# The start of a two-layer decoder trunk: products of zeros first, weights by k-tile, small parameters later, a fixed order in the first unit

## The chip, the cores and the metric

The kernel runs on one core of a Trainium2 chip. The metric is the device time of one execution in microseconds (us); the median over several runs is compared. Times inside an execution are counted from the start of the profiled span. Engines are named as in the profile: PE (matrix products; PEld is its weight load), DVE (vector), ACT (activation), POOL, SP (here it only issues transfers).

## The reference, cut to what matters

x is 256 tokens by 1024 features in float32. Two layers follow each other, each of the form below; the mixer is differential attention in layer 0 and a Mamba-2 SSD mixer in layer 1.

```python
h = h + 0.5 * swiglu(rmsnorm(h, ffn1_norm[i]), ffn1_w_gate[i], ffn1_w_up[i], ffn1_w_down[i])
...
h = h + diff_attention(...)      # layer 0; ssd_mixer(...) in layer 1
h = h + memory_cross_attention(rmsnorm(h, xa_norm[i]), mem, ...)
h = h + 0.5 * swiglu(rmsnorm(h, ffn2_norm[i]), ffn2_w_gate[i], ffn2_w_up[i], ffn2_w_down[i])
...
return rmsnorm(h, final_norm)
```

`swiglu(h, g, u, d)` is `(silu(h @ g) * (h @ u)) @ d` with a hidden width of 2816. All that the change touches lies in the first feed-forward block of layer 0 and in what is loaded for later stages.

## The kernel before, in words

Every large product is worked in units. A unit multiplies the activations, 256 tokens held as two halves of 128, by 512 (or 256) columns of weights, over the 1024 features in eight k-tiles of 128. To keep float32 accuracy, both sides are split in a high and a low part, and each product is three matmuls: high by high (L209), high by low weights (L210), low activations by high weights (L211). One unit of 512 columns has 8 k-tiles x 2 halves x 3 = 48 matmuls of 128x512.

Weights arrive through SP in tiles `w` of four k-tiles, 1 MB each (class `W`, L142 to L159), into four buffers. A granule (`Gran`, L161 to L182) covers two k-tiles of them: `split` has ACT copy the high part (`whi`, L180), and DVE subtract it to get the low part (`wlo`, L181; in some later units POOL). High and low parts have four buffers each, and `use` splits two granules ahead of the one that PE works on (`AHEAD = 2`).

The activations are turned by `Norm.turn` (L321): PE transposes 128x128 pieces of `h` (L327) into PSUM tiles `xt`, two k-tiles to a tile, then ACT writes the high part `xh` scaled by the norm's gain (L282), and DVE the low part `xl` (L283). ACT and DVE read one `xt` tile in turn, not at the same time. `square` (L311) sums the squares on ACT for the root mean square, which is first used when the first gate product is evacuated (L521).

The written order is that of a small planner, `Pipe`: each granule moves its clock on by an estimate of PE's time, and `pipe.after(us, f)` writes the instructions of `f` once the clock is there. After that, the compiler's scheduler orders each engine's instructions anew by its own estimates. Engines then work strictly in that order, so that an instruction that waits holds up all that stands behind it on its engine.

At the outset (`begin`, L364): ACT's queue loads the identity and the first gains (L88, L90). SP loads the left half of x (`load_x(0)`: two transfers of 256 KB), 512 KB of the first gate weights (k-tiles 0 and 1), the right half of x, then the other gate weights in pieces of 512 KB, then the up weights. POOL's queue loads five small parameter arrays (L99, L384 to L392): `cst` (masks and rope frequencies), `pos` (positions), `rows` (gains of all later norms), `vec` (SSD parameters) and `lqk` (the lambda vectors of the attention). What needs them is written much later (`rope_tables`, L463; `lam_col`, L451; `nega`, L889), but the scheduler sets some of it very early.

Of the kernel before, what the change touches and what calls it, by code (L numbers as in the profile page):

```python
# [15 lines left out]
P = 128  # L16
# [42 lines left out]
def trunk(ctx, tc, a, out):  # L59
# [34 lines left out]
    def load_x(c):  # L94
        for t in range(2):
            nc.sync.dma_start(h[t][c], a["x"][0, t * P:(t + 1) * P, c * 512:(c + 1) * 512])
    load_x(0)
    cst = const.tile([P, C_W - P], F32, name="cst")
    nc.gpsimd.dma_start(cst, a["cst"][:, P:])  # L99
    triu = cst[:, C_TRIU - P:C_TRIU]  # L100
# [134 lines left out]

    def wide(parts, norm, name, fin, eng=None):
# [15 lines left out]
        units.append(([Gran(k, 2, *((w[k // 4], 0, n) for w, (_, _, n) in zip(ws, parts)),  # L252
                            eng=eng if k == 6 else None) for k in range(0, KT, 2)], run))

# [46 lines left out]
    class Norm:  # L301
# [9 lines left out]
        def square(self, c):  # L311
# [4 lines left out]
            if self.n == 2:  # L316
                s = sm.tile([P, 16], F32, name="nsum", tag="nsum")
                nc.vector.tensor_tensor(s[:, 0:2], self.ss[:, 0:2], self.ss[:, 2:4], op=ALU.add)
                self.col = rpow(s[:, 0:2], 1.0 / D, 2, "rcol")

        def turn(self, c):  # L321
            for i in range(2):
                ps = v2(small_ps("xt"))
                for j in range(2):
                    f = (2 * i + j) * P
                    for t in range(2):
                        nc.tensor.transpose(ps[:, j, t * P:(t + 1) * P], h[t][c][:, f:f + P], ident)  # L327
                for j in range(2):
                    k = 4 * c + 2 * i + j
                    xh = xp.tile([P, S], F32R, name="xh", tag="xh")  # L330
                    xl = xp.tile([P, S], F32R, name="xl", tag="xl")
                    split_act(xh, xl, ps[:, j, :], self.g[:, k:k + 1])
                    self.x.append((xh, xl))

# [28 lines left out]

    def begin(norm):  # L364
        ps0 = small_ps("pcol0")
        nc.tensor.transpose(ps0[:, :KT + 1], rows0, ident[:KT + 1, :KT + 1])
        nc.vector.tensor_copy(cols0, ps0[:, :KT + 1])
        first = units[0][0]
        w0, w1 = first[0].parts[0][0], first[2].parts[0][0]
# [13 lines left out]
    pos_i = const.tile([P, 2], I32, name="pos")  # L383
    nc.gpsimd.dma_start(pos_i, a["positions"][0].rearrange("(t p) -> p t", p=P))  # L384
    rows12 = slot("rows12")[:, :2 * P].rearrange("p (i c) -> p i c", i=2)
    nc.gpsimd.dma_start(rows12, a["rows"].rearrange("(i p) c -> p i c", p=P))
    rowpos = {nm: r for nm, r, _ in _rows()}
    vec = const.tile([P, 96], F32, name="vec")
    nc.gpsimd.dma_start(vec, a["vec"][0:96].partition_broadcast(P))
    dtb, alog, dsk = vec[:, 0:32], vec[:, 32:64], vec[:, 64:96]  # L390
    lqk = slot("lqk")[:, 0:256]
    nc.gpsimd.dma_start(lqk, a["vec"][96:352].partition_broadcast(P))  # L392
    lqk = lqk.rearrange("p (k d) -> p k d", k=4)
# [57 lines left out]
    def lam_col():  # L451
        pr = work("lampr", 128).rearrange("p (c d) -> p c d", c=2)
        l4 = lqk.rearrange("p (c t) d -> p c t d", t=2)
        nc.vector.tensor_tensor(pr, l4[:, :, 0, :], l4[:, :, 1, :], op=ALU.mult)
        nc.vector.tensor_reduce(lam[:, 0:2], pr, axis=AX.X, op=ALU.add)
# [7 lines left out]
    def rope_tables():  # L463
# [4 lines left out]
        posf = sm.tile([P, 16], F32, name="posf", tag="posf", bufs=1)  # L468
        v.tensor_copy(posf[:, 0:2], pos_i)
        inv = cst[:, C_INV - P:C_INV - P + 32]  # L470
# [41 lines left out]
    def ffn_hidden(nm, l, norm, extra=None):  # L512
# [33 lines left out]
        def turn(us, n):  # L546
            for i in range(0, n // P, 2):
# [8 lines left out]
                for j in range(2):  # L556
                    hid.append((hi[:, j, :], lo[:, j, :]))
        wg, wu = a[nm + "_w_gate"][l], a[nm + "_w_up"][l]
        for c in range(HID // 512):
            wide([(wg, c * 512, 512)], norm, "gate", gate_fin(c))  # L560
            wide([(wu, c * 512, 512)], norm, "up", up_fin(c))
# [277 lines left out]
    def ssd(norm, nxt, kv):  # L839
# [38 lines left out]
        def dt_fin(pd):  # L878
# [9 lines left out]
            nega = const.tile([P, 32], F32, name="nega")  # L888
            nc.scalar.activation(nega, alog, AF.Exp)  # L889
            v.tensor_scalar(s, u, 2.0, None, op0=ALU.add)  # L890
# [360 lines left out]
```

## Time and profile before

| | |
|---|---|
| median of 3 runs | 1337.58 us (1336.15 to 1338.41) |
| the profiled execution: time | 1336.94 us |
| the profiled execution: span from first to last instruction | 1335.1 us |
| PE busy | 1301.0 us, 97% of the span |
| DVE, ACT, POOL busy | 63%, 53%, 9% |
| mean granted TensorE clock | 0.996 |

The 1.84 us between the execution's time and its span lie outside the first and last instruction. A row of the timeline has the start, the time, the engine, the line, what is written from what, the count and, in brackets, how long the engine was idle before it and what released it. Two matmuls overlap in their records, so the distance between two starts is what one costs in a row of them. In the windows view each engine's busy time in a stretch is followed by the granted clock (PEclk), the share of the DMA engines and the rate in GB/s.

### The profile page before, as it was taken

Reading aid. Unit: us, or ns where it says so; the run is one execution under the profiler, and the core shown is the slowest. Engines: PE = TensorE matmul, PEld = TensorE weight load, DVE = VectorE, ACT = ScalarE, POOL = GpSimd, SP = SyncE. Lnnn points to the kernel's source line nnn. Section 1 sums busy time; section 2 is a strip of 40 time slices with the busy share of each in tenths; the row PEclk is TensorE's granted clock in tenths of the full one; section 3 lists DMA queues with packets and bytes.
Section 4 is the critical chain, followed back from the end, with each engine's and each line's share of the span. In section 5 each row is a group of like instructions: output and inputs, shape, how many; then the busy total and the mean of one; then the engine's idle time right before and its main releaser. Section 6 shows DMA issues by size and latency. Waiting matters only on the chain.

```text
span 1335.1 us, 17775 instructions
## 1 busy us (share of the span) xinstructions
PE 1301.0 (97%) x6991; PEld 1115.8 (84%) x6991; DVE 842.7 (63%) x1207; ACT 714.2 (53%) x1125; POOL 115.0 (9%) x109
## 2 busy tenths in 40 slices
PE   6999999999999999999999999988999999999997
PEld 5888888778988888888888889988897898888886
DVE  5555457876566555555556456998988675655553
ACT  5445544676455544444445445767756564644432
POOL 1000002200000000000000001444423000000000
PEclk9999999999999999999999999999999999999999
DMA  8564555334535554655555546634544544555551
GB/s 268 191 218 155 195 203 177 126 130 152 190 128 177 173 194 133 221 193 201 189 187 175 191 149 231 225 118 135 169 145 156 177 158 151 193 177 174 204 174 48
DMA packets 133254, 232.01 MB, mean 174 GB/s; under 512 B 5273, under 2 KB 32066, under 8 KB 133170
## 3 DMA queue, kind: packets, MB, share of 16 engines
q1 hardware_dynamic: 132496, 229.56, 52.2%
q0 software_dynamic: 368, 0.98, 0.3%
q8 instruction: 55, 0.90, 0.3%
q10 hardware_dynamic: 306, 0.33, 0.1%
q14 instruction: 29, 0.24, 0.1%
HBM read 229.77 MB, written 1.08 MB: 173 GB/s over the span
## 4 chain that ended last, share of the span: by engine, by line
PE 85%; DVE 9%; ACT 2%; POOL 2%; DMA 1%; issue 1%; POOLq 0%; DVEq 0%; ACTq 0%; SPq 0%
PE out L211 7%; PE out L210 7%; PE out L209 7%; PE gate L210 6%; PE gate L211 6%; PE gate L209 5%; PE up L209 5%; PE up L210 5%; PE up L211 5%; DVE wlo L181 2%; PE fin L209 1%; PE fin L211 1%; PE fin L210 1%; PE htp L551 1%; DVE xs L953 1%; PE mv L209 1%
## 5 line engine op out<-in xcount | busy, mean ns | idle before, releaser
L181 DVE TENSOR_TENSOR wlo<-w,whi 128x1024 fp32r<-128x1024 f32 (+1 forms) x440 | 522.9, 1194 | 408.6 <-ACT whi L180 407.6
L180 ACT CAST whi<-w 128x1024 fp32r<-128x1024 f32 (+1 forms) x444 | 446.8, 1012 | 461.4 <-PE out L211 142.5
L210 PE MATMUL gate<-wlo,xh 128*128 128x512 f32 x320 | 126.1, 394 | 2.2 <-DVE wlo L181 2.2
L209 PE MATMUL gate<-whi,xh 128*128 128x512 f32 x320 | 127.6, 400 | 0.0
L211 PE MATMUL gate<-whi,xl 128*128 128x512 f32 x320 | 125.8, 393 | 0.0
L209 PE MATMUL up<-whi,xh 128*128 128x512 f32 x320 | 124.6, 389 | 0.0
L211 PE MATMUL up<-whi,xl 128*128 128x512 f32 x320 | 124.6, 389 | 0.0
L210 PE MATMUL up<-wlo,xh 128*128 128x512 f32 x320 | 124.6, 389 | 0.0
L209 PE MATMUL out<-whi,hid_hi 128*128 128x512 f32 x264 | 103.6, 393 | 0.0
L211 PE MATMUL out<-whi,hid_lo 128*128 128x512 f32 x264 | 102.9, 390 | 0.0
L210 PE MATMUL out<-wlo,hid_hi 128*128 128x512 f32 x264 | 102.8, 390 | 0.0
L210 PEld LDWEIGHTS gate<-wlo,xh 128*128 128x128 f32 x320 | 60.9, 190 | 14.9 <-DVE wlo L181 3.0
L211 PEld LDWEIGHTS gate<-whi,xl 128*128 128x128 f32 x320 | 60.8, 190 | 12.6
L209 PEld LDWEIGHTS gate<-whi,xh 128*128 128x128 f32 x320 | 60.9, 191 | 12.0
L209 PEld LDWEIGHTS up<-whi,xh 128*128 128x128 f32 x320 | 60.1, 188 | 12.4
L211 PEld LDWEIGHTS up<-whi,xl 128*128 128x128 f32 x320 | 60.1, 188 | 12.4
L210 PEld LDWEIGHTS up<-wlo,xh 128*128 128x128 f32 x320 | 60.1, 188 | 12.4
L290 POOL TENSOR_TENSOR rcol<-msq,neghalf 128x2 f32<-128x2 f32 x8 | 5.6, 700 | 700.4 <-DVE msq L288 700.4
L211 PEld LDWEIGHTS out<-whi,hid_lo 128*128 128x128 f32 x264 | 49.6, 188 | 10.4
L210 PEld LDWEIGHTS out<-wlo,hid_hi 128*128 128x128 f32 x264 | 49.6, 188 | 10.0
L209 PEld LDWEIGHTS out<-whi,hid_hi 128*128 128x128 f32 x264 | 49.6, 188 | 10.0
L209 PE MATMUL fin<-whi,hid_hi 128*128 128x512 f32 (+1 forms) x110 | 38.3, 348 | 0.0
(352 smaller groups left out, 2777.9 us busy)
## 6 DMA issues: line engine op xcount, KB each, us to landing
w<-in_ffn_w_up_dram SPq DMA_DIRECT2D x40, 1024.0 KB, 5.0
w<-in_ffn_w_down_dram SPq DMA_DIRECT2D x40, 1024.0 KB, 5.1
w<-in_ffn_w_gate_dram SPq DMA_DIRECT2D x38, 1024.0 KB, 5.0
w<-in_ssd_w_in_dram SPq DMA_DIRECT2D x24, 1024.0 KB, 5.2
w<-in_xa_w_kv_dram SPq DMA_DIRECT2D x16, 1024.0 KB, 4.9
w<-in_da_w_in_dram SPq DMA_DIRECT2D x12, 1024.0 KB, 5.0
w<-in_xa_w_q_dram SPq DMA_DIRECT2D x8, 1024.0 KB, 5.0
w<-in_xa_w_o_dram SPq DMA_DIRECT2D x8, 1024.0 KB, 5.0
```

The lines of the kernel that those rows point to most:

```text
L180: nc.scalar.copy(hv, src)
L181: self.eng.tensor_tensor(self.lo[:, :, o:o + n], src, hv.bitcast(F32), op=ALU.subtract)
L209: nc.tensor.matmul(o, lhsT=lh, rhs=rh, start=start, stop=False)
L210: nc.tensor.matmul(o, lhsT=lh, rhs=rl, start=False, stop=False)
L211: nc.tensor.matmul(o, lhsT=ll, rhs=rh, start=False, stop=stop)
L290: nc.gpsimd.tensor_tensor(c[:, :n], m[:, :n], neghalf[:, :n], op=ALU.pow)
L551: nc.tensor.transpose(tp[:, j, t * P:(t + 1) * P], us[t][:, (i + j) * P:(i + j + 1) * P], ident)
L953: v.scalar_tensor_tensor(o[:, j, d:], raw[:, j, :S - d], tap(k), o[:, j, d:], op0=ALU.mult, op1=ALU.add)
```

## The change

1. DVE sets a tile `warm` of 128x512 float32 to zero at the very start, and PE, ahead of everything else, multiplies it nine times by itself, read as bf16 (128x128 by 128x512). The results are not used.
2. The first gate weights are loaded by k-tile (256 KB each): k-tiles 0 and 1 ahead of x's second half, then k-tiles 2 and 3; k-tiles 4 to 7 in two pieces as before.
3. The first unit has granules of one k-tile for k-tiles 0 to 3 (`single=True`) and of two after that; POOL makes the low part of k-tile 3. In these four k-tiles the matmuls come in the order high by high, low activations by high weights, high by low weights, for both halves of the tokens each.
4. The transposes are written apart (`flip`) from the splits (`put`), and the splits of activations and weights alternate. The second half of x is turned after two k-tiles of products, not ahead of them.
5. The five small parameter loads move from POOL's queue to SP's, behind the first half of the up weights (`load_params`, written 8.0 us into the planner's clock). Their first users (`posf`, `lampr`, `nega`) keep their written place.
6. The first unit and what is ahead of it keep the written order on PE, DVE, ACT and SP (`manual_schedule`); the rest is left to the scheduler as before. The squares of x are written 9.5 us into the planner's clock, in the place of 9.0.

```diff
+    warm = slot("warm")
+    nc.vector.memset(warm, 0.0)
...
-        begin(first_norm)
-        for gs, f in units:
+        with tc.manual_schedule(engines={E.PE, E.DVE, E.Activation, E.SP}):
+            begin(first_norm)
+            for gs, f in units[:1]:
+                f(*gs)
+        for gs, f in units[1:]:
...
+                    if single and kt < 4:
+                        for i, (l, r) in enumerate(((xh, g.hi), (xl, g.hi), (xh, g.lo))):
+                            for t in range(2):
+                                nc.tensor.matmul(ps[t], lhsT=l[:, t * P:(t + 1) * P], rhs=r[:, k, :],
+                                                 start=kt == 0 and i == 0, stop=False)
+                        pipe.pe(1.36)
+                        continue
...
+        cut = ((0, 1), (1, 1), (2, 1), (3, 1), (4, 2), (6, 2)) if single else ((0, 2), (2, 2), (4, 2), (6, 2))
...
     def begin(norm):
+        for _ in range(9):
+            nc.tensor.matmul(small_ps("warm"), lhsT=warm.bitcast(BF16)[:, :P], rhs=warm.bitcast(BF16)[:, :512], start=True, stop=True)
...
-        w0.load(0, 2)
+        w0.load(0, 1)
+        w0.load(1, 1)
         load_x(1)
-        w0.load(2, 2)
+        w0.load(2, 1)
+        w0.load(3, 1)
         w1.load(0, 2)
         w1.load(2, 2)
-        norm.turn(0)
-        first[0].split()
-        norm.turn(1)
-        pipe.after(9.0, lambda: [norm.square(c) for c in range(2)])
+        for i in range(2):
+            ps = norm.flip(0, i)
+            for j in range(2):
+                k = 2 * i + j
+                norm.put(k, ps[:, j, :])
+                if k < 3:
+                    first[k].split()
+        done[0] = 3
+        def second():
+            a = [norm.flip(1, i) for i in range(2)]
+            norm.put(4, a[0][:, 0, :])
+            ready(5)
+            for k in (5, 6, 7):
+                norm.put(k, a[k // 2 - 2][:, k % 2, :])
+        pipe.after(2.7, second)
+        pipe.after(9.5, lambda: [norm.square(c) for c in range(2)])
+        pipe.after(8.0, load_params)
...
+    def load_params():
+        nc.sync.dma_start(cst, a["cst"][:, P:])
+        nc.sync.dma_start(pos_i, a["positions"][0].rearrange("(t p) -> p t", p=P))
+        nc.sync.dma_start(rows12, a["rows"].rearrange("(i p) c -> p i c", p=P))
+        nc.sync.dma_start(vec, a["vec"][0:96].partition_broadcast(P))
+        nc.sync.dma_start(lqk2, a["vec"][96:352].partition_broadcast(P))
```

Three places show the moves. First DVE at the outset, before: ahead of the first `xl` (low part of an x tile) stand the rope tables (`posf` to `whole`) and the lambda product `lampr`, which wait for parameters.

```order
L367 COPY cols_95<-pcol_133 128x9 [waits PE_49]
L469 CAST posf<-pos 128x2 [waits DMASW1_49]
...
L488 TENSOR_SCALAR frac<-part 128x64
L454 TENSOR_TENSOR lampr<-lqk 128x128 [waits DMASW4_49]
L491 SCALAR_TENSOR_TENSOR frac<-part,frac 128x64 [waits DVE_49]
L489 TENSOR_SCALAR whole<-frac 128x64 [waits DVE_49]
L455 TENSOR_REDUCE lam<-lampr 128x2 [waits DVE_49]
L283 SCALAR_TENSOR_TENSOR xl<-xt,cols_95,xh 128x256 [waits Activation_49]
```

The same place after the change:

```order
L100 MEMSET warm 128x512
L391 COPY cols_96<-pcol_150 128x9 [waits PE_49]
L460 TENSOR_SCALAR cols_96<-cols_96 128x1 [waits DVE_49]
L298 SCALAR_TENSOR_TENSOR xl<-xt,cols_96,xh 128x256 [waits Activation_49]
L183 TENSOR_TENSOR wlo<-w,whi 128x512 [waits DMAHW4_49,Activation_49]
L298 SCALAR_TENSOR_TENSOR xl<-xt,cols_96,xh 128x256 [waits Activation_49]
L183 TENSOR_TENSOR wlo<-w,whi 128x512 [waits DMAHW5_49,Activation_49]
```

The rope and lambda work has left the outset of DVE (it now stands in the following units), and the low parts of x and of the weights alternate.

Second, ACT at the outset after the change. Before, the table load carried no wait, since the first activation behind it was a square of x; now the squares stand behind the first unit's splits, and the table load waits for the gain column `cols` on DVE.

```order
L88 DMA ident<-in_cst_dram 128x128
L90 DMA rows_83<-in_rows_dram 9x128
L297 ACT_TABLE_LOAD [waits DVE_49]
L297 ACTIVATE xh<-xt,cols_96 128x256 [waits PE_49]
L182 CAST whi<-w 128x512 [waits DMAHW4_49]
L297 ACTIVATE xh<-xt,cols_96 128x256 [waits DVE_49]
L182 CAST whi<-w 128x512 [waits DMAHW5_49]
```

So the first `xh` now stands behind a table load that itself waits. Third, SP after the change, from the first half of the up weights on: the five parameter loads stand between the two halves, and each waits for an earlier transfer to have landed.

```order
L160 DMA w<-in_ffn_w_up_dram 128x4x512 [waits DMAHW4_49]
L448 DMA cst<-in_cst_dram 128x288 [waits DMAHW5_49]
L449 DMA pos<-in_positions_dram 128x2x1 [waits DMAHW6_49]
L450 DMA rows_99<-in_rows_dram 128x2x128 [waits DMAHW7_49]
L451 DMA vec<-in_vec_dram 128x96 [waits DMAHW0_49]
L452 DMA lqk<-in_vec_dram 128x256 [waits DMAHW1_49]
L160 DMA w<-in_ffn_w_up_dram 128x4x512 [waits DMAHW2_49]
```

Before, the two halves of the up weights stood next to each other. Elsewhere, ACT gains two table loads around the moved lambda exponential in the first block, and one up matmul stands in the last third of the first gate unit; the order of the rest is the same but for single swaps.

More of the change, by code (lines that the diff above doesn't have):

```diff
@@ L234, in proj, with wide @@
             units.append(([Gran(k, 4, (ws[k // nk], 256 * i, 256), eng=eng if k and not i else None) for k in (0, 4)], run))
-    def wide(parts, norm, name, fin, eng=None):
+    def wide(parts, norm, name, fin, eng=None, single=False):
         ws = [[W(src, k, 4, c0, n) for k in range(0, KT, 4)] for src, c0, n in parts]
@@ L251, in run @@
             fin(ps)
-        units.append(([Gran(k, 2, *((w[k // 4], 0, n) for w, (_, _, n) in zip(ws, parts)),
-                            eng=eng if k == 6 else None) for k in range(0, KT, 2)], run))
+        cut = ((0, 1), (1, 1), (2, 1), (3, 1), (4, 2), (6, 2)) if single else ((0, 2), (2, 2), (4, 2), (6, 2))
+        units.append(([Gran(k, nk, *((w[k // 4], 0, n) for w, (_, _, n) in zip(ws, parts)),
+                            eng=eng if k == (3 if single else 6) else None) for k, nk in cut], run))
     def out_b(src, nkt, lhs, fin, both=False):
@@ L319, in square, with flip, put @@
                 self.col = rpow(s[:, 0:2], 1.0 / D, 2, "rcol")
+        def flip(self, c, i):
+            ps = v2(small_ps("xt"))
+            for j in range(2):
+                f = (2 * i + j) * P
+                for t in range(2):
+                    nc.tensor.transpose(ps[:, j, t * P:(t + 1) * P], h[t][c][:, f:f + P], ident)
+            return ps
+        def put(self, k, ps):
+            xh = xp.tile([P, S], F32R, name="xh", tag="xh")
+            xl = xp.tile([P, S], F32R, name="xl", tag="xl")
+            split_act(xh, xl, ps, self.g[:, k:k + 1])
+            self.x.append((xh, xl))
         def turn(self, c):
             for i in range(2):
-                ps = v2(small_ps("xt"))
+                ps = self.flip(c, i)
                 for j in range(2):
[L325 to L333, printed above, removed]
+                    self.put(4 * c + 2 * i + j, ps[:, j, :])
         def add(self, c):
@@ L368, in begin @@
         first = units[0][0]
[L369 to L370 removed]
+        w0, w1 = first[0].parts[0][0], first[4].parts[0][0]
+        w0.load(0, 1)
+        w0.load(1, 1)
         load_x(1)
[L372 removed]
+        w0.load(2, 1)
+        w0.load(3, 1)
         w1.load(0, 2)
         w1.load(2, 2)
[L375 to L378 removed]
+        for i in range(2):
+            ps = norm.flip(0, i)
+            for j in range(2):
+                k = 2 * i + j
[12 more added lines that the diff above has]
+        pipe.after(8.0, load_params)
     first_norm = nrm = Norm(cols0)
     pos_i = const.tile([P, 2], I32, name="pos")
[L384 removed]
     rows12 = slot("rows12")[:, :2 * P].rearrange("p (i c) -> p i c", i=2)
[L386 removed]
     rowpos = {nm: r for nm, r, _ in _rows()}
     vec = const.tile([P, 96], F32, name="vec")
[L389 removed]
     dtb, alog, dsk = vec[:, 0:32], vec[:, 32:64], vec[:, 64:96]
     lqk = slot("lqk")[:, 0:256]
[L392 removed]
+    lqk2 = lqk
     lqk = lqk.rearrange("p (k d) -> p k d", k=4)
@@ L558, in ffn_hidden @@
         wg, wu = a[nm + "_w_gate"][l], a[nm + "_w_up"][l]
+        first = {} if units else dict(single=True, eng=nc.gpsimd)
         for c in range(HID // 512):
-            wide([(wg, c * 512, 512)], norm, "gate", gate_fin(c))
+            wide([(wg, c * 512, 512)], norm, "gate", gate_fin(c), **first)
+            first = {}
             wide([(wu, c * 512, 512)], norm, "up", up_fin(c))
@@ L888, in dt_fin @@
             nega = const.tile([P, 32], F32, name="nega")
-            nc.scalar.activation(nega, alog, AF.Exp)
+            tc.keep_in_program_order(nc.scalar.activation(nega, alog, AF.Exp))
             v.tensor_scalar(s, u, 2.0, None, op0=ALU.add)
```

6 lines of the change are left out of this document (3 added, 3 removed).

## The prediction

> **What bounds the kernel now.** I read the busy times by stretch first, then the timeline of the first 40 us, the transfers with their time to landing, the groups by shape, and last the granted clock where PE stands still. Busy time by stretch, with columns PE, PEld, DVE, ACT, POOL (count in brackets), then PEclk, DMA share, GB/s:
>
> ```profile
> 0.00:20.00 20.00, 9.64 (x29) 7.07 (x30) 9.72 (x40) 10.78 (x22) 5.42 (x15) 1.00 0.91 289
> 20.00:40.00 20.00, 20.00 (x88) 16.53 (x87) 13.02 (x23) 10.77 (x15) 0.00 (x0) 1.00 0.74 239
> 40.00:200.00 160.00, 160.00 (x741) 132.84 (x740) 85.90 (x93) 80.80 (x109) 0.71 (x1) 1.00 0.58 190
> ```
>
> From 20 us on PE is the bound: busy for all of 160 us in the third row, DVE and ACT about half of it. Only the outset has room: 9.64 of 20 us busy. What comes earlier there is worth its full length at the end, since PE has no later gap in this block to lose it in. The outset in detail:
>
> ```profile
> 0.74 0.86 SPq L96 DMA_DIRECT2D h<-in_x_dram  x2
> 1.81 1.28 ACT L314 ACT_TABLE_LOAD   x1 [1.81 <-issue]
> 4.16 0.24 PE L366 MATMUL pcol<-ident,rows 9*128 9x9 f32 x1 [4.16 <-DMA rows<-in_rows_dram]
> 4.34 1.97 PE L327 MATMUL xt<-ident,h 128*128 128x128 f32 x8
> 4.44 0.17 DVE L367 COPY cols<-pcol 128x9 f32<-128x9 f32 x1 [4.44 <-PE pcol L366]
> 8.90 1.05 ACT L180 CAST whi<-w 128x1024 fp32r<-128x1024 f32 x1 [2.12 <-DMA w<-in_ffn_w_gate_dram]
> 12.12 0.29 DVE L454 TENSOR_TENSOR lampr<-lqk 128x128 f32<-128x128 f32 x1 [2.30 <-DMA lqk<-in_vec_dram]
> 12.15 1.20 PE L209 MATMUL gate<-whi,xh 128*128 128x512 f32 x2
> 12.76 0.47 DVE L283 SCALAR_TENSOR_TENSOR xl<-xt,cols,xh 128x256 fp32r<-128x256 f32 x1
> 14.31 1.22 DVE L181 TENSOR_TENSOR wlo<-w,whi 128x1024 fp32r<-128x1024 f32 x1
> 15.58 0.79 PE L210 MATMUL gate<-wlo,xh 128*128 128x512 f32 x1 [2.23 <-DVE wlo L181]
> 20.01 1.05 PE L209 MATMUL gate<-whi,xh 128*128 128x512 f32 x2
> 20.87 0.49 PE L210 MATMUL gate<-wlo,xh 128*128 128x512 f32 x1
> 21.20 0.39 PE L211 MATMUL gate<-whi,xl 128*128 128x512 f32 x1
> 28.70 0.39 PE L209 MATMUL up<-whi,xh 128*128 128x512 f32 x1
> 28.93 0.39 PE L210 MATMUL up<-wlo,xh 128*128 128x512 f32 x1
> ```
>
> Four losses stand here. The first weights reach ACT at 8.90. DVE stands behind `lqk` until 12.12, so `xl` comes at 12.76 and `wlo` at 14.31. PE is gapless only from 15.58. And from there its products cost 0.43 us each (20.01 to 20.87 for two), and from 21.20 on less; 28.70 to 28.93 is 0.23. PEclk prints 1.00 here all the same, so I read the clock from these distances: half before about 21.0, full after. The up unit's second product starts at 28.93; this is my milestone, as behind it PE works without a gap.
>
> **The parts, one by one.** Prices by shape (busy us, mean ns), the issues of `lqk` and of the last piece of the first gate weights, and single transfers (KB, us from issue to landing; the first is that piece):
>
> ```profile
> L282 ACT ACTIVATE xh<-xt,cols 128x256 fp32r<-128x256 f32 x64 | 28.3, 469 | 13.7 <-DVE xl L283 12.1 <-PE xt L327 1.4
> L181 DVE TENSOR_TENSOR wlo<-w,whi 128x512 fp32r<-128x512 f32 x33 | 21.4, 688 | 14.7 <-ACT whi L180 14.7
> L180 ACT CAST whi<-w 128x512 fp32r<-128x512 f32 x33 | 18.9, 619 | 20.3 <-PE up L211 18.6 <-PE out L211 1.7
> L181 POOL TENSOR_TENSOR wlo<-w,whi 128x1024 fp32r<-128x1024 f32 x4 | 9.6, 2405 | 33.4 <-ACT whi L180 33.4
> ```
>
> ```profile
> 4.01 0.55 POOL L392 DMA_DIRECT2D lqk<-in_vec_dram  x1
> 4.58 1.23 SPq L158 DMA_DIRECT2D w<-in_ffn_w_gate_dram  x1
> ```
>
> ```profile
> w<-in_ffn_w_gate_dram SPq DMA_DIRECT2D x1, 512.0 KB, 11.1
> cst<-in_cst_dram POOLq DMA_DIRECT2D x1, 144.0 KB, 4.5
> rows<-in_rows_dram POOLq DMA_DIRECT2D x1, 128.0 KB, 7.6
> vec<-in_vec_dram POOLq DMA_DIRECT2D x1, 48.0 KB, 7.3
> lqk<-in_vec_dram POOLq DMA_DIRECT2D x1, 128.0 KB, 8.1
> pos<-in_positions_dram POOLq DMA_DIRECT2D x1, 1.0 KB, 6.0
> ```
>
> *Zero products.* No row shows DVE's memset; its bounds are 0 and the 0.69 of `wlo` on the same shape. I take 0.55, as a write without reads; with the engines' start at 0.74 (SP's first issue), PE begins at 1.3. Nine products at the half clock's 0.43 last until 5.2. They delay `pcol` from 4.16 to 5.2, and `cols` from 4.61 (4.44 + 0.17) to 5.65: a cost of 1.0.
>
> *The table load.* It was done by 3.1 and now waits for `cols`: 5.7 to 7.0. That puts 1.28 on the path (nothing at best, if its wait passed to the activation). Eight transposes (1.97) run from 5.2 to 7.2; the first `xh` needs the first four, so it goes at 7.0.
>
> *First k-tile.* `xh` 7.0 to 7.45, `whi` (0.62) to 8.05, `xl` to 8.0, `wlo` (0.69) to 8.75. First product at 8.1, in place of 12.15. With two splits per k-tile on DVE (0.48 + 0.69 = 1.17, less some overlap) and on ACT (0.47 + 0.62 = 1.09), each k-tile takes less than its six products at the full clock (1.36), so PE is the bound as long as transfers are there. POOL's `wlo` of k-tile 3 is half of 2405 ns, 1.2 us from 11.3 to 12.5; PE needs it at 14.0.
>
> *Transfers.* Ahead of k-tile 0's weights now stand 512 KB, ahead of k-tile 1's 768. The rate bounds are a stretch with the small parameters beside it and one without:
>
> ```profile
> 6.00:8.00 2.00, 0.30 (x2) 0.00 (x0) 0.00 (x0) 0.78 (x3) 0.38 (x2) 1.00 1.22 299
> 12.00:14.00 2.00, 1.35 (x5) 0.63 (x3) 1.88 (x12) 0.73 (x3) 0.00 (x0) 1.00 1.05 406
> ```
>
> x's first half was there by about 4.7, as eight transposes of it ran from 4.34. At 299 GB/s each further 256 KB takes 0.88: k-tile 0's weights 5.6, k-tile 1's 6.5, x's second half 8.2, k-tiles 2 and 3 9.1 and 10.0, 4 and 5 11.7, 6 and 7 13.5, first half of up 17.0. At 406 GB/s the last is 13.8. ACT wants them at 7.4, 8.5, (PE) 10.8, 9.4, 10.7, 11.7, 15.3 and 16.2, so only the last can be late. It matters, since one up product stands ahead of the gate unit's last eleven: up's first `whi` at 17.0 + 1.05, then twelve products, is 20.8. Cost 0 to 0.7; I take 0.3.
>
> *The rest of the first unit.* From 8.1: 48 products and the one up product that stands among them, 49 x 0.227 = 11.1, and eight transposes, 0.9 at the full clock (half of 1.97). That gives 20.1; with 0.3 for transfers, 20.4 for the up unit's second product. Before: 28.93. **Gain 8.5.**
>
> *What is late next.* ACT now does the four squares (0.63 each) behind the splits, then the table load for Silu, which waits for the unit's end:
>
> ```profile
> 14.00 0.63 ACT L314 ACTIVATE sq<-h 128x512 f32<-128x512 f32 x1
> 28.26 1.28 ACT L521 ACT_TABLE_LOAD   x1 [0.99 <-PE gate L211]
> 29.56 0.69 ACT L521 ACTIVATE gs<-gate,rcol 128x512 f32<-128x512 f32 x1
> ```
>
> Table load 20.7 to 22.0, `gs` to 22.8, `whi` of up's k-tiles 4 and 5 to 23.8, its `wlo` (1.22) to 25.0; PE wants it at 25.6. The margin is 0.6; beyond it each us is lost once. I take nothing, and 0.5 at the other end. The moved rope and lambda work (some 33 small DVE operations like the `cols` copy of 0.17, two table loads of 1.28 on ACT) falls into the stretch where DVE and ACT are busy 86 and 81 of 160 us, beside splits made two granules (24 products, 5.4 us) ahead: nothing.
>
> *Parameters on SP.* 449 KB (the five rows) stand ahead of the second half of up, 2.6 by itself at 406 GB/s. They take 1.1 at that rate, or, as the longest row has it, 8.1: the second half lands between 13.8 + 1.1 + 2.6 = 17.5 and 24.5. ACT wants it at 22.8, so the cost is 0 to 1.7 less the margin of 0.6; I take nothing, since at 4.01 + 8.1 all five had landed with x and the first weights beside them.
>
> The sum is made against the profiled execution: 1336.94 - 8.5 = 1328.4, span 1326.6. It lay 0.64 below the median, so the median becomes 1337.58 - 8.5 = **1329.1**.
>
> **When the clock opens.** The sum has it open by 8.1. The stall at 892.6 shows how it moves:
>
> ```profile
> 892.00:896.00 4.00, 0.64 (x6) 0.43 (x4) 3.41 (x7) 2.31 (x7) 2.63 (x4) 0.86 0.13 46
> 896.00:900.00 4.00, 2.67 (x12) 2.50 (x12) 3.53 (x6) 3.19 (x9) 1.90 (x2) 0.50 0.11 8
> 900.00:904.00 4.00, 4.00 (x18) 3.22 (x17) 3.88 (x9) 2.21 (x4) 0.09 (x1) 0.79 0.71 254
> 897.33 1.17 PE L1073 MATMUL ty<-ident,y 128*128 128x128 f32 x4 [4.69 <-DVE y L1066]
> ```
>
> 0.86 over 4 us is 1.1 us at half, so from 894.9; 0.79 is 1.7 us, so until 901.7. The half clock came 2.3 us after PE went idle and ended 4.4 after its work at 897.33; at the outset it ended 5.4 after 15.58. In the new outset PE works gapless from 1.3 to 7.2, 5.9 us, which is longer than both; the gap to 8.1 is 0.9, shorter than 2.3. Hence open. The Trainium skill (TensorE: Matmul & The Clock Gate, Part 1: The HAM clock gate) says that the clock opens after one whole busy window of about 3.4 us, and that the windows run freely. The 6.8 us at half agree, being two such windows. By that rule nine zero products alone (3.9) hold a whole window in about one start in seven, and with the transposes (5.9) in about three of four, as an estimate from that page.
>
> **The rivals.** *The clock opens late* (zeros don't count as work, or the release falls in the gap). For: no row shows a product of zeros. Against: the 5.9 us above. Then it opens 5.4 after 8.1, at 13.5, and the products until then cost double: 2.7 more, of which PE's later waits take 0.2. Gain 6.0: 1331.6. The page's rule, where it misses, is this rival.
>
> *Transfers as slow as before.* If the last gate piece still lands at 4.58 + 11.1 = 15.7, up's first MB lands 2.6 later at 406 GB/s, at 18.3; its `whi` is done at 19.4, and with the twelve products behind it (2.7) the milestone is 22.1. Gain 6.8: 1330.8. For: the first weights alone kept ACT waiting until 8.90. Against: the five loads of POOL's queue are no longer beside them.
>
> *The change doesn't do what it says.* The early start is eaten where the order is new (up's k-tiles 4 to 7, or the stalls near 890 with `nega` now beside them): under 2.7 left, about 1336.5.
>
> *Slower.* The five parameter loads hold SP's queue one after the other. By their rows that would be 4.5 + 6.0 + 7.6 + 7.3 + 8.1 = 33.5, and up's second half lands at 13.8 + 33.5 + 2.6 = 49.9; with its splits (2.3) PE stands from 25.6 to 52.2. 26.6 lost, 8.5 won: 1355.7. It turns into a loss from a hold of 15 on (22.8 + 8.5 - 16.4). Against: the last, issued at 4.01, had landed by 12.1, so they overlap.
>
> **How the numbers follow.** Forecast 0.64, late clock 0.17, slow transfers 0.12, no effect 0.03, slower 0.04. A measurement of this kernel can tell 0.2%, 2.7 us, from no change; the first three cases are all faster by more: 0.93, 0.03, 0.04. The range: at the low end the table load off the path (1.28 more) and half of the spread of the runs (1336.15 to 1338.41, 1.1): 1326.7. At the high end the late clock and the same half, 1332.7, rounded up: 1332.8.
>
> **What would show it.** Right: nine zero products 0.43 apart from about 1.3; a table load near 5.7; first gate product near 8.1 and products 0.23 apart from there; up's second product near 20.4; PE gapless to 40. Wrong: products 0.43 apart beyond 9 us (late clock); `whi` waiting for transfers (slow transfers); a PE wait in up's k-tiles 4 to 7, for the table load chain if under 1 us, for the parameters if many.

## The result and the profile after

The changed kernel takes 1328.35 us in the median of 4 runs (1327.82 to 1328.70), the kernel before on the same chip 1337.99 (1336.15 to 1338.42): the ratio is 0.9929 with a 95% interval from 0.9918 to 0.9941. The profiled execution took 1328.16 with a span of 1326.3, against 1336.94 and 1335.1 before. So 8.8 us went from one profile to the other, and 9.6 from median to median.

Busy time by stretch, after (columns as before: PE, PEld, DVE, ACT, POOL, PEclk, DMA share, GB/s):

```profile
0.00:20.00 20.00, 17.05 (x73) 11.89 (x74) 10.69 (x18) 11.98 (x22) 2.76 (x10) 1.00 0.90 302
20.00:40.00 20.00, 20.00 (x95) 16.65 (x94) 12.64 (x17) 12.65 (x17) 0.70 (x1) 1.00 0.84 302
40.00:200.00 160.00, 160.00 (x742) 132.90 (x741) 91.09 (x130) 84.46 (x117) 0.71 (x2) 1.00 0.58 191
```

PE is busy for 17.05 of the first 20 us, where it was 9.64 (3.95 of the new 17.05 are zeros, from 1.46 to 5.41 in the next view). From 20 us on it has no gap, as before. DVE's 91.09 against 85.90 in the third row is the moved rope and lambda work, and PE does not wait for it. The outset in the timeline of after:

```profile
1.46 4.02 PE L388 MATMUL warm<-warm 128*128 128x512 bf16 x9 [1.46 <-DVE warm L100]
5.41 0.27 PE L390 MATMUL pcol<-ident,rows 9*128 9x9 f32 x1
5.61 1.19 PE L342 MATMUL xt<-ident,h 128*128 128x128 f32 x8
5.97 1.28 ACT L297 ACT_TABLE_LOAD   x1 [5.97 <-DVE cols L391]
7.26 0.47 ACT L297 ACTIVATE xh<-xt,cols 128x256 fp32r<-128x256 f32 x1
7.64 0.61 ACT L182 CAST whi<-w 128x512 fp32r<-128x512 f32 x1
8.30 0.73 PE L257 MATMUL gate<-whi,xh 128*128 128x512 f32 x2 [1.49 <-ACT whi L182]
8.86 0.62 PE L257 MATMUL gate<-whi,xl 128*128 128x512 f32 x2
9.33 0.63 PE L257 MATMUL gate<-wlo,xh 128*128 128x512 f32 x2
20.62 0.39 PE L216 MATMUL up<-wlo,xh 128*128 128x512 f32 x1
```

Eight transposes that took 1.97 take 1.19, and from the first gate product two stand in 0.46 to 0.56, where before two took 0.85. So the clock is full at 8.30 (the trace's clock record has it open at 5.86), and the table load is back on the path, behind `cols`. The milestone, the up unit's second product, stands at 20.62 instead of 28.93: 8.31 earlier. Matched products stay 8.3 to 8.4 us ahead from there on (1306.72 against 1298.38 near the end, 8.34), with the same stalls between. What is left to the span's 8.8 is 0.44 behind the last product.

What was to be late next, in the timeline of after:

```profile
21.06 1.28 ACT L565 ACT_TABLE_LOAD   x1
24.01 2.36 DVE L183 TENSOR_TENSOR wlo<-w,whi 128x1024 fp32r<-128x1024 f32 x2 [2.57 <-ACT whi L182]
```

The first of these two low parts is done near 25.2 (forecast 25.0), and PE does not wait. The stall near 890 came 8.4 earlier and kept its two windows at half the clock, 6.8 us, as the granted clock shows (before the group 888 to 892 stands 0.81, behind it 0.83):

```profile
888.00:892.00 4.00, 3.03 (x12) 2.83 (x13) 3.41 (x7) 3.05 (x8) 1.63 (x2) 0.50 0.14 9
```

### The profile page after: what moved, and what is told of

Its sections match the earlier page's. It is cut to its first block, busy times and chain, and to the rows that moved or that the text cites. A ratio compares the mean times of both kernels' runs of the same rounds, so it can differ in the third digit from the quotient of the medians.

```text
span 1326.3 us, 17804 instructions
## 1 busy us (share of the span) xinstructions
PE 1300.0 (98%) x7000; PEld 1114.1 (84%) x7000; DVE 843.4 (64%) x1209; ACT 716.0 (54%) x1129; POOL 113.5 (9%) x105
## 4 chain that ended last, share of the span: by engine, by line
PE 86%; DVE 8%; ACT 2%; POOL 2%; issue 1%; DMA 0%; POOLq 0%; DVEq 0%; ACTq 0%
PE out L217 7%; PE out L216 7%; PE out L215 7%; PE up L215 5%; PE up L216 5%; PE up L217 5%; PE gate L216 5%; PE gate L217 5%; PE gate L215 5%; DVE wlo L183 2%; PE fin L215 1%; PE fin L217 1%; PE fin L216 1%; PE htp L595 1%; DVE xs L999 1%; PE mk L215 1%
## 5 line engine op out<-in xcount | busy, mean ns | idle before, releaser
L183 DVE TENSOR_TENSOR wlo<-w,whi 128x1024 fp32r<-128x1024 f32 (+2 forms) x441 | 522.5, 1191 | 398.6 <-ACT whi L182 397.2
L215 PE MATMUL gate<-whi,xh 128*128 128x512 f32 x312 | 123.3, 395 | 0.0
L216 PE MATMUL gate<-wlo,xh 128*128 128x512 f32 x312 | 121.9, 391 | 0.0
L217 PE MATMUL gate<-whi,xl 128*128 128x512 f32 x312 | 121.7, 390 | 0.0
```

Of the source, the lines that this page charges most:

```text
L183: self.eng.tensor_tensor(self.lo[:, :, o:o + n], src, hv.bitcast(F32), op=ALU.subtract)
L215: nc.tensor.matmul(o, lhsT=lh, rhs=rh, start=start, stop=False)
L216: nc.tensor.matmul(o, lhsT=lh, rhs=rl, start=False, stop=False)
L217: nc.tensor.matmul(o, lhsT=ll, rhs=rh, start=False, stop=stop)
```

## The experiments

Three theories stood against each other on where the 8.3 us come from: (1) DVE's stand behind `lqk`; (2) the parameter transfers that run beside the first weights; (3) the new order with the open clock that the zeros bring. Kernels were made with parts alone and with parts undone. The table has the milestone, the time at which the clock record goes to full (both from the one profiled execution), the median and the ratio to before on the same chip.

| kernel | milestone | clock opens | median (runs) | ratio, 95% |
|---|---|---|---|---|
| before | 28.93 | 21.07 | 1337.99 (4) | 1 |
| before, users late | 24.79 | 15.65 | 1333.17 (6) | 0.9967 [0.9955, 0.9980] |
| before, users late and loads moved | 22.12 | 12.25 | 1330.10 (4) | 0.9952 [0.9936, 0.9969] |
| before with zeros | 28.98 | 4.20, again 21.27 | 1337.49 (10) | 0.9995 [0.9986, 1.0005] |
| changed | 20.62 | 5.86 | 1328.35 (4) | 0.9929 [0.9918, 0.9941] |
| changed, once more | 20.64 | 5.77 | 1328.57 (5) | 0.9926 [0.9914, 0.9939] |
| changed without zeros | 20.77 | 10.06 | 1328.85 (4) | 0.9932 [0.9915, 0.9949] |
| the same, once more | 20.93 | 10.53 | 1328.68 (5) | 0.9928 [0.9916, 0.9940] |
| changed, loads moved back | 22.15 | 7.03 | 1330.77 (4) | 0.9946 [0.9931, 0.9961] |
| changed, loads back, no zeros | 23.97 | 14.91 | 1331.32 (4) | 0.9954 [0.9940, 0.9969] |
| changed, order left free | 20.09 | 6.76 | 1327.60 (4) | 0.9922 [0.9907, 0.9937] |
| changed, table load early | 20.18 | 7.13 | 1328.44 (4) | 0.9929 [0.9914, 0.9944] |
| changed, five zeros, order free | 22.24 | 13.10 | 1329.42 (4) | 0.9940 [0.9923, 0.9958] |
| changed, table early, zeros split | 21.12 | 10.46 | 1328.89 (5) | 0.9925 [0.9913, 0.9938] |

Two columns are of one execution each, and this limits what they can tell. All changes of the clock within a profile lie whole windows of 3.413 us apart, and where these windows begin differs between executions: with the same zeros from 1.46 to 5.41 the clock opened at 5.86, 5.77, 6.76, 7.03 and 7.13. One window more or less at half the clock is worth up to half of its length, 1.7 us, at the milestone. Smaller differences there hold for the executions shown.

**The zeros undone.** The memset and the nine products are left out.

```diff
-    warm = slot("warm")
-    nc.vector.memset(warm, 0.0)
...
-        for _ in range(9):
-            nc.tensor.matmul(small_ps("warm"), lhsT=warm.bitcast(BF16)[:, :P], ...)
```

> The changed kernel without the nine products of zeros and their memset. My theory (the zeros open PE's clock by the time the real products begin): the gain column comes 1.2 us earlier, but the first weights land near 7.0 whatever PE does, so the first gate product moves only from 8.3 to about 7.6 to 8.0; its products then stand 0.43 us apart until about 12 to 13.5, and the up unit's second product falls at 22.0 to 22.7 in place of 20.6. Time about 1330.2 (1329.7 to 1330.8). Rival (the zeros open nothing, the transposes and first products would do it as well): the clock is open at 8 us without them, and the kernel is 0.3 to 1.0 faster than the changed one, near 1327.6.

PE's part of the timeline of this kernel:

```profile
6.97 1.22 PE L255 MATMUL gate<-whi,xh 128*128 128x512 f32 x2 [0.53 <-ACT whi L180]
7.99 1.05 PE L255 MATMUL gate<-whi,xl 128*128 128x512 f32 x2
8.84 1.05 PE L255 MATMUL gate<-wlo,xh 128*128 128x512 f32 x2
9.69 0.81 PE L255 MATMUL gate<-whi,xh 128*128 128x512 f32 x2
20.77 0.39 PE L214 MATMUL up<-wlo,xh 128*128 128x512 f32 x1
```

The first product comes 1.33 earlier (6.97), at half the clock; two cost 0.85 until the clock opens at 10.06, in the fourth pair. The milestone is only 0.15 later. Neither theory had this: the opening came 3.1 after the first product and not 5.4, and the earlier start pays for most of what the half clock costs. The same kernel was run once more for the spread.

> The changed kernel without the zeros, once more, for the spread. Theory A (windows run freely, so without zeros the clock opens anywhere from 3.1 to 6.5 after the first product): another profile opens it at another time, milestone 20.7 to 22.4, and the runs lie between 1328.3 and 1330.7, the median 0.5 to 1.5 above the changed kernel's in the same job. Theory B (the time to the opening is fixed by the work): open again at 10.0 to 10.2, milestone 20.7 to 20.9, runs within 0.5 of 1328.9.

It opened at 10.53, 3.58 behind the first product at 6.95, milestone 20.93, median 1328.68, runs 1328.43 to 1329.67. The opening and the milestone lie outside the second theory's ranges and inside the first's; the median lies only 0.1 above the changed kernel's in that job, where the first theory had 0.5 or more. Beside it on the chip the changed kernel itself:

> The changed kernel itself, once more, beside the three others. Theory A (zeros and transposes leave PE full from 1.46 to 6.8, which holds a whole window in most starts): clock open between 5 and 8, milestone 20.4 to 20.9, median 1327.8 to 1328.8, most runs within 1 of each other. Theory B (the zeros do nothing for the spread): runs spread as widely as without them, over 2 us.

It gave the same outset again (milestone 20.64, clock open at 5.77), median 1328.57 and runs from 1327.58 to 1330.04. So in this outset nine products of zeros win 0.15 and 0.29 at the milestone in the profiles, and the medians (1328.35 and 1328.57 with them, 1328.85 and 1328.68 without) do not tell them from nothing. That the zeros narrow the spread is not shown either: 2.5 with them, 1.2 without, in that job.

**The parameter loads moved back to POOL's queue at the outset,** their users left late.

```diff
+    nc.gpsimd.dma_start(cst, a["cst"][:, P:])
...
+    nc.gpsimd.dma_start(lqk, a["vec"][96:352].partition_broadcast(P))
...
-        pipe.after(8.0, load_params)
```

> The changed kernel with the five parameter loads back on POOL's queue at the outset; their users keep their late place. My theory (they hold up the first transfers): first weights land near 8, the last gate piece near 15.7, up's first half near 18.5 as before the change, and the up unit's second product falls at 22.3 to 23.2; time about 1330.5 (1329.8 to 1331.2). Rival (what cost time before was DVE standing behind the lambda vectors, not the transfers themselves): the same as the changed kernel within 0.4, 1328.4.

Two rows of its timeline:

```profile
11.73 0.62 ACT L183 CAST whi<-w 128x512 fp32r<-128x512 f32 x1 [2.08 <-DMA w<-in_ffn_w_gate_dram]
22.15 0.39 PE L217 MATMUL up<-wlo,xh 128*128 128x512 f32 x1
```

ACT waits 2.08 for the weights of k-tile 2, and the milestone is 1.53 later, a little less than the first theory had. The median, 2.4 above the changed kernel's, lies in that theory's range and not in the rival's. The profiled time (1331.53) is 3.37 above, and the half of it that is not from the outset goes with two windows at half the clock that the changed kernel's first profile has not (290.3 to 293.7, 928.6 to 932.0).

**Loads moved back and no zeros:** what is left is the order of weights and splits, with late users (the edits of both kernels above together).

> The changed kernel without the zeros and with the five parameter loads back on POOL's queue at the outset (their users late): what is left is the load order by k-tile, the splits by k-tile and the kept order. Theory A (the waits cover each other: a late transfer of k-tile 2 is hidden by a half clock): milestone near 22.2, as with the loads moved back alone, 1330.3 to 1331.8. Theory B (late first weights also move the opening of the clock): milestone 23.5 to 24.5, 1332.3 to 1333.8.

ACT waits at both early weights, in its timeline:

```profile
8.12 0.62 ACT L181 CAST whi<-w 128x512 fp32r<-128x512 f32 x1 [1.81 <-DMA w<-in_ffn_w_gate_dram]
12.63 0.62 ACT L181 CAST whi<-w 128x512 fp32r<-128x512 f32 x1 [2.63 <-DMA w<-in_ffn_w_gate_dram]
23.97 0.39 PE L215 MATMUL up<-wlo,xh 128*128 128x512 f32 x1
```

The milestone fits the second theory (late weights also put off the clock, to 14.91), the median of 1331.32 the first: the two did not agree. Against the kernel with late loads and no zeros (20.77) the loads cost 3.20 here, twice the 1.53 that they cost with the zeros. The medians do not show this doubling: they lie 2.5 apart here (1331.32 and 1328.85) and 2.4 with the zeros (1330.77 and 1328.35). In this profile the clock opened 6.1 behind the first product (8.79), against 3.1 and 3.6 with late loads, so a part of the 3.20 may be where the windows fell.

**The users of the parameters alone,** in the kernel before: only their written place is kept, the loads stay on POOL's queue.

```diff
-        nc.vector.tensor_tensor(pr, l4[:, :, 0, :], l4[:, :, 1, :], op=ALU.mult)
+        tc.keep_in_program_order(nc.vector.tensor_tensor(pr, l4[:, :, 0, :], l4[:, :, 1, :], op=ALU.mult))
...
-        v.tensor_copy(posf[:, 0:2], pos_i)
+        tc.keep_in_program_order(v.tensor_copy(posf[:, 0:2], pos_i))
```

(`nega` in the same way.)

> The kernel before with the users of the parameters alone kept in their written place; the loads stay on POOL's queue at the outset. Theory A (the stall of DVE behind lqk is the larger half, the transfers the smaller): first whi at 8.9 as before, first wlo done near 11.2, milestone near 25: 1333.5 to 1335.0, about 1 slower than with the loads moved too. Theory B (the transfers are the bound, DVE's stall is covered by them): milestone within 1 of 28.93 and 1336.5 to 1338.5.

DVE, ACT and PE in its timeline:

```profile
6.23 0.48 DVE L283 SCALAR_TENSOR_TENSOR xl<-xt,cols,xh 128x256 fp32r<-128x256 f32 x1 [1.48 <-ACT xh L282]
8.73 1.05 ACT L180 CAST whi<-w 128x1024 fp32r<-128x1024 f32 x1 [1.92 <-DMA w<-in_ffn_w_gate_dram]
9.81 1.23 DVE L181 TENSOR_TENSOR wlo<-w,whi 128x1024 fp32r<-128x1024 f32 x1 [3.10 <-ACT whi L180]
13.50 1.04 ACT L180 CAST whi<-w 128x1024 fp32r<-128x1024 f32 x1 [1.76 <-DMA w<-in_ffn_w_gate_dram]
24.79 0.39 PE L210 MATMUL up<-wlo,xh 128*128 128x512 f32 x1
```

`xl` stands at 6.23 instead of 12.76 and the first `wlo` at 9.81 instead of 14.31. Half of the whole gain is there: 4.14 at the milestone. What holds up now are the weights: ACT waits for them at 8.73 and at 13.50. (Milestone and median, 1333.17, are a little better than the first theory had them, and far from the second.)

**Users late and the loads moved** behind up's first half on SP's queue: the parameter part of the change, whole, in the kernel before.

```diff
-    nc.gpsimd.dma_start(cst, a["cst"][:, P:])
...
+        pipe.after(8.0, load_params)
```

> The kernel before with the parameter part alone: the five loads go to SP's queue behind the first half of up, and their users keep their written place. No zeros, old load order, old granules, scheduler's order. Theory A (the parameters were the main loss at the outset): DVE no longer stands until 12.12, the first whi comes earlier than 8.90 since nothing small is beside it, the first wlo is done near 10 in place of 15.5, and up's second product stands near 23.5 in place of 28.93: 1332.2 to 1334.2. Theory B (most of the gain comes from the load and split order): the first product and wlo still wait for the 512 KB pieces, milestone 26 or later: over 1335.

The same rows:

```profile
7.02 1.05 ACT L179 CAST whi<-w 128x1024 fp32r<-128x1024 f32 x1 [0.28 <-DMA w<-in_ffn_w_gate_dram]
9.92 1.04 ACT L179 CAST whi<-w 128x1024 fp32r<-128x1024 f32 x1
22.12 0.39 PE L209 MATMUL up<-wlo,xh 128*128 128x512 f32 x1
```

ACT comes to the weights 1.7 and 3.6 earlier (the second time it no longer waits), the milestone is 2.67 earlier, and the median of 1330.10 is 2 better than even the theory that favoured it, though one of its four runs took 1333.85. The transfers of the first 9 us show that these small loads weigh more than their size. With the loads at the outset (users late alone), queue, packets, MB and share of the DMA engines' time:

```profile
q1 hardware_dynamic: 852, 1.60, 51.5%
q0 software_dynamic: 147, 0.33, 24.2%
```

`q0` carries POOL's loads: 0.33 MB took 24.2% of the engines' time, 73% for each MB, and x and the weights 32%. This need not be POOL's queue alone. In the changed kernel the same arrays come through SP's queue, behind the first weights, and land between 15.7 and 18.7. There too the engines are busy (0.91) and move little (232 GB/s); in the stretch ahead of this one, 11 to 14 us, it was 405 GB/s at 1.05:

```profile
14.00:17.00 3.00, 3.00 (x15) 2.49 (x14) 2.01 (x5) 1.72 (x3) 0.53 (x2) 1.00 0.91 232
```

PE is busy for all 3 us of it. That points to the time at which the loads run rather than to their queue, but it is not shown: no kernel here moved them in time alone or to the other queue alone.

**The zeros alone,** in the kernel before.

```diff
+    nc.vector.memset(warm, 0.0)
...
+        for _ in range(9):
+            nc.tensor.matmul(small_ps("warm"), lhsT=warm.bitcast(BF16)[:, :P], ...)
```

> The kernel before with the nine products of zeros alone. Theory A (the clock is set by how full PE was in windows of 3.4 us): it opens near 6 behind the zeros, but PE then idles for about 3 us until x's second half is there at 9.5, and again for 2.2 behind the first products at 12.15; the clock is back at half before 15.58 and opens again between 17 and 21. Milestone 27.2 to 29.0, 1336.0 to 1338.5. Theory B (once opened it stays open over gaps of 3 us): products 0.23 apart from 15.58, milestone 26.2, 2.7 won: 1334.8 to 1335.6.

PE in its timeline:

```profile
5.00 1.09 PE L329 MATMUL xt<-ident,h 128*128 128x128 f32 x8
8.71 0.41 PE L329 MATMUL xt<-ident,h 128*128 128x128 f32 x2 [2.62 <-DMA h<-in_x_dram]
12.15 1.54 PE L329 MATMUL xt<-ident,h 128*128 128x128 f32 x6 [3.03 <-DMA h<-in_x_dram]
13.34 1.20 PE L211 MATMUL gate<-whi,xh 128*128 128x512 f32 x2
28.98 0.39 PE L212 MATMUL up<-wlo,xh 128*128 128x512 f32 x1
```

The clock opened, at 4.20, and was lost again, as the first theory had it: it was still full for the two transposes at 8.71 (0.41; the same two took 0.69 before), and six take 1.54 at 12.15, what they took before. The milestone did not move, and the ratio's interval holds 1. But the edit did more than add zeros. The scheduler now set the gain column `cols` on DVE behind the early rope work, which waits for `pos`, so the first `xh` came at 10.18 in place of 5.70:

```profile
10.18 0.47 ACT L284 ACTIVATE xh<-xt,cols 128x256 fp32r<-128x256 f32 x1 [4.81 <-DVE cols L371]
```

Also the last of x came later (12.15, before 10.95). So this run shows that the clock is lost again in such a gap, and not what zeros alone are worth in the old order.

**The kept order undone:** the scheduler orders the first unit as all others.

```diff
-        with tc.manual_schedule(engines={E.PE, E.DVE, E.Activation, E.SP}):
-            begin(first_norm)
-            for gs, f in units[:1]:
-                f(*gs)
+        begin(first_norm)
+        for gs, f in units[:1]:
+            f(*gs)
```

> The changed kernel without the kept order in the first unit; the scheduler orders it, and sets the squares of x among the first splits on ACT, the table load ahead of all waits. My theory (the order matters little once the parameters' users are late): four squares of 0.6 more on ACT's path, the table load's 1.3 less; the up unit's second product at 20.2 to 21.6, time 1328 to 1329.4. Rival (the kept order is a main part of the gain): second up product beyond 22.5, time 1330.5 or more.

ACT and PE in its timeline:

```profile
1.81 1.28 ACT L328 ACT_TABLE_LOAD   x1 [1.81 <-issue]
6.33 0.62 ACT L182 CAST whi<-w 128x512 fp32r<-128x512 f32 x1 [2.12 <-DMA w<-in_ffn_w_gate_dram]
7.38 0.73 PE L256 MATMUL gate<-whi,xh 128*128 128x512 f32 x2
20.09 0.39 PE L215 MATMUL up<-wlo,xh 128*128 128x512 f32 x1
```

The scheduler puts a square and so the table load ahead, and `whi` ahead of `xh`; the first product is 0.92 earlier, the milestone 0.53. With the users late, keeping the order wins nothing: 1327.60 is the lowest median of all, though its interval overlaps the change's.

**The table load early,** with the order kept: an activation of 16 zeros per partition stands ahead on ACT.

```diff
+        early = sm.tile([P, 16], F32, name="early", tag="early", bufs=1)
+        nc.scalar.activation(early, warm[:, 0:16], AF.Square)
```

> The changed kernel with one small square of the zero tile on ACT (128x16, result unused) ahead of the first split, so that the table load no longer waits for the gain column. Theory A (the table load's 1.28 us lies on the path): first gate product near 7.0, time about 1327.1. Theory B (behind it the first weights' landing near 7.0 takes over): table load done by about 3, first high part of x near 6.2, first high part of the weights waits until about 7.0, first product near 7.6 to 8.0; gain only 0.3 to 0.6, time 1327.8 to 1328.1.

The milestone is 20.18: 0.44 of the load's 1.28 come back. The first product (7.80) is 0.50 earlier, as `xh` now waits until 6.76 for the transposes, which stand behind the zeros:

```profile
5.61 1.81 PE L342 MATMUL xt<-ident,h 128*128 128x128 f32 x8
6.76 0.47 ACT L297 ACTIVATE xh<-xt,cols 128x256 fp32r<-128x256 f32 x1 [3.44 <-PE xt L342]
```

But in this execution the clock opened only at 7.13, so the transposes ran at half of it and took 1.81, where the changed kernel's own profile has 1.19. So the two profiles differ in more than the load. In the median nothing is seen (1328.44).

**Five zeros in place of nine, order free.**

> The changed kernel with the scheduler's order in the first unit and five zero products in place of nine, so that they end near 3.6, ahead of pcol's data at 4.1. Theory A (pcol and the splits come 1.1 earlier and the transposes behind the zeros still keep the clock open): first product near 6.9 limited by the transfer of k-tile 0, milestone 19.6 to 19.9, 1326.8 to 1327.5. Theory B (five zeros don't fill a window, the clock opens near 10 as without zeros): products 0.43 apart until then, milestone 20.3 to 20.8, 1327.8 to 1328.9.

PE in its timeline:

```profile
1.46 2.32 PE L387 MATMUL warm<-warm 128*128 128x512 bf16 x5 [1.46 <-DVE warm L100]
3.88 0.24 PE L389 MATMUL pcol<-ident,rows 9*128 9x9 f32 x1
7.39 1.22 PE L256 MATMUL gate<-whi,xh 128*128 128x512 f32 x2 [0.60 <-ACT whi L182]
11.82 1.05 PE L256 MATMUL gate<-wlo,xh 128*128 128x512 f32 x2
22.24 0.39 PE L215 MATMUL up<-wlo,xh 128*128 128x512 f32 x1
```

`pcol` is earlier, but two products still cost 0.86 at 11.82, and the clock opens at 13.10, 5.7 behind the first product. Against the same kernel with nine zeros (20.09) the milestone is 2.15 later. Both theories fell short of this profile: it is worse than those of no zeros at all in the kept order (20.77 and 20.93). But it is one execution (1329.84) of four that lie far apart, from 1326.87, the fastest run of any kernel here, to 1331.84. So five zeros do harm in some executions, and not in all.

**Six zeros ahead and two behind the transposes,** table load early, order kept: the version that the theory of full windows would make best.

```diff
-        for _ in range(9):
+        for _ in range(6):
...
+            if i == 1:
+                pw = small_ps("warm")
+                for _ in range(2):
+                    nc.tensor.matmul(pw, lhsT=warm.bitcast(BF16)[:, :P], ...)
```

> The changed kernel with the table load early and the zeros split: six products ahead of pcol (done by 4.1, when its data is there) and two behind the transposes of x's first half, in the gap before the first product. Theory A (what counts is that PE is full for a window, and that zeros delay nothing): clock open by 8, first product 7.0 to 7.5, milestone 19.4 to 19.9, 1327.2 to 1327.9, and runs close together. Theory B (a wait of 0.5 for x's second tile among the transposes spoils the window, as with five zeros): clock opens near 10, milestone 20.3 to 21.0, 1328.2 to 1329.2.

First product at 7.13, as hoped, but the clock opens at 10.46 and the milestone is 21.12, 0.94 later than with nine zeros in one piece and the same table load. The second theory held, with the milestone just beyond its 21.0 and the median (1328.89) inside its range; that the wait for x among the transposes (0.29 here) is the cause is not shown.

## Why the prediction was right

The predicted median was 1329.1 (1326.7 to 1332.8); 1328.35 came. The forecast's chain held, with the steps up to the first product 0.2 to 0.3 late:

| step | forecast | measured |
|---|---|---|
| zeros from, `pcol` | 1.3, 5.2 | 1.46, 5.41 |
| table load | 5.7 | 5.97 |
| first gate product | 8.1 | 8.30 |
| from there to the milestone | 12.3 | 12.32 |
| milestone | 20.4 | 20.62 |
| gain there | 8.5 | 8.31 |
| profiled time | 1328.4 | 1328.16 |

That 12.3 came out as 12.32 is in part luck. The 49 products were priced right (0.227 apart where nothing holds them up). The eight transposes took 0.8 in place of 0.9. The 0.3 booked for a late transfer was lost, but not there: the first half of up had landed in time, and near 0.4 went at four steps, two where the first product of a row took 0.32 to 0.34 and two around 17.7, where the one up product waited for ACT's splits.

*What bounds the kernel.* That the outset's time is worth its full length at the end was right: 8.31 at the milestone, 8.34 near the end. In the experiments too the milestone and the profiled time move together against before: users late 4.14 and 1336.94 - 1332.95 = 3.99, users and loads 6.81 and 6.98, loads back without zeros 4.96 and 5.05. Two fall short, both by 1.4, loads moved back (6.78 and 5.41) and the changed kernel's second profile (8.29 and 6.90): these are the two that lost the clock for a window near 290, told below.

*The four losses.* Parts were taken out in two orders, and the milestones give their sizes. From before to after: users late 4.14 (28.93 to 24.79), loads moved 2.67 (to 22.12), the new order 1.35 (to 20.77), zeros 0.15 (to 20.62). From the other side: with the order new and no zeros the loads are worth 3.20 (23.97 to 20.77), and the new order with loads at the outset 0.82 (24.79 to 23.97). The medians, each against before on its own chip, give 4.7, 3.1, 1.6 and 0.2 for the first four. A part of each is the clock, which opens earlier at each step (21.07, 15.65, 12.25, 10.06, 5.86); no run separates it. So the parameters, which the change has "behind", carry 6.8 of 8.3, and the items that it puts ahead 1.5. The prediction's sum ran along the new timeline and so had the whole right without saying this.

*The transfers.* The shape was right and two times were low. The single loads of the gate weights at the outset, KB and time to landing, with those of up:

```profile
w<-in_ffn_w_gate_dram SPq DMA_DIRECT2D x4, 256.0 KB, 5.6
w<-in_ffn_w_gate_dram SPq DMA_DIRECT2D x2, 512.0 KB, 7.5
w<-in_ffn_w_up_dram SPq DMA_DIRECT2D x2, 1024.0 KB, 8.4
lqk<-in_vec_dram SPq DMA_DIRECT2D x1, 128.0 KB, 8.5
```

The weights of k-tiles 0 and 1 landed at 6.95 and 7.6 by their issue and time, where 5.6 and 6.5 stood, and those of k-tiles 2 and 3 at 9.6 and 10.1 (9.1 and 10.0). K-tile 2's came as ACT did (9.54) and the others before it, so this cost nothing; without zeros ACT waited 1.00 for k-tile 2. The first half of up came at 6.92 + 8.4 = 15.3, inside 13.8 to 17.0. `lqk` landed at 18.7, and the second half of up was no wait for PE: the rival by which parameters hold SP's queue did not come, as they overlap here too.

*What was mis-sized.* The table load was booked at 1.28 on the path. It stands there, but taking it off gave 0.44 at the milestone, in an execution whose transposes ran at half the clock and held `xh` until 6.76. In the changed kernel's own profile the four transposes that `xh` needs end near 6.4, so up to 0.9 of the load may count there; no run shows it. The zeros were booked as a cost of 1.0 against a late clock of 2.7. Where the clock did come late in spite of zeros (the profile of five of them), 2.15 were lost: that rival was real and nearly of its size. But leaving the zeros out isn't that rival, since the work then starts 1.33 earlier, and the clock opens 3.1 and 3.6 after it. Net the zeros were worth 0.15 to 0.29 at the milestone in these profiles.

*The clock.* "Open by 8.1, by 5.9 us without a gap" was right in both profiles of the changed kernel (5.86 and 5.77), and in the three other kernels with nine zeros and the new loads (6.76, 7.03 and 7.13, all ahead of the first product). That 5.9 us without a gap is enough in every start is not shown: five profiles are few, and five or six zeros, with gaps of 0.3 to 0.6 behind them, missed. The Trainium skill (TensorE: Matmul & The Clock Gate, Part 1: The HAM clock gate) has windows of about 3.4 us that run freely, and the clock open after a busy one; how full that must be it does not say. The records agree on the windows: the changes of the clock in one profile lie whole multiples of 3.413 us apart (258 of them from 5.86 to 886.50 in the changed kernel's first profile, 256 from 21.07 to 894.9 before). Read as a full window, as in the prediction, that rule of the Trainium skill does not fit the kernel without zeros, which opened at 10.06 though the window from 6.64 held 0.3 of idle time: there the measurement decides.

## What to carry to other kernels

At the start, look first for an in-order engine that waits for something nobody needs yet: work on DVE that waited for parameters (the rope tables and the lambda product), set early by the scheduler, was half of the gain, and the small loads beside the first weights a third. Zeros that open PE's clock bring little where they also delay the work behind them: here the clock opened 4.2 us earlier and the first product came 1.33 later. A gap of 3 us behind them lost the clock again. Size a part by undoing it and by doing it alone: the first named part of this change was worth at most 0.3 of 8.3 us at the milestone. Then look whether the part that was done alone changed something else too, as with the gain column here.

## What was not expected of the hardware

*How full a window must be.* A window of 3.41 us before the clock's opening held 3.41 us of busy PE in most profiles, but 3.09 without zeros (all products) and 2.75 in the kernel before with zeros (0.79 to 4.20, all zeros). Windows that did not open it held 2.71 (products, loads back and no zeros), 2.82 and 2.79 (five zeros; with transposes among them) and 3.13 (six zeros and two; mostly transposes). So busy time alone does not decide. Transposes may count less than products; no run here tells that apart, and it stays open. Windows of 1.87 to 1.92 busy did not close the open clock (behind the opening in both profiles of the changed kernel and in the kernel before with zeros), one of 0.41 did (7.62 to 11.03 in the latter). Busy times here are sums over the records of PE between two changes of the clock, taken in steps of 3.413.

*What parts two runs of one kernel.* The two profiles of the changed kernel have the same outset to 0.02 us, and times of 1328.16 and 1330.04. Up to 252 us matched products lie within 0.06 of each other, at 302 they are 1.69 apart. The second profile's stretch between:

```profile
286.00:290.00 4.00, 2.93 (x10) 1.97 (x11) 3.83 (x9) 3.82 (x9) 0.00 (x0) 0.88 0.66 245
290.00:294.00 4.00, 4.00 (x18) 3.32 (x17) 0.44 (x1) 1.05 (x1) 0.00 (x0) 0.69 0.71 237
```

PE has a short gap there in both, but only the second lost the clock for one window, 289.1 to 292.5; half of 3.41 is 1.7. So whether a gap costs such a window differs between executions of one kernel, and the 1.7 is nearly all that lies between the medians of the last four versions in the table (1327.60 to 1329.42). That the spread of the other runs comes from this too is not shown: only profiled executions have a trace.
